# One transformer pair on one core: the first down projection by one level of Strassen's product, with weight sums made in DRAM

## The chip, the core and the metric

The kernel runs on one core of one Trainium2 chip. The metric is the device time of one execution in microseconds (us), the median of repeated executions. TensorE (PE) does the matrix products, VectorE (DVE) and ScalarE (ACT) the work on tiles, GpSimd (POOL) small side work, and the queue of SyncE (SP) issues every transfer of the kernel before. In the trace, PE is the matmul side of TensorE and PEld its loading of stationary operands.

## What is computed

Two blocks run one after the other on 512 tokens of width 1024 in float32. The first holds attention of 12 heads and a state-space mixer side by side; the part that matters here is its feed-forward at the end, and the attention at its start, because transfers of the change stand there.

```
f = rmsnorm(h, norm_ffn_pre_w[layer])
f = jnp.square(jax.nn.relu(f @ w_up[layer])) @ w_down[layer]      # 1024 -> 4096 -> 1024
h = h + rmsnorm(f, norm_ffn_post_w[layer])
```

The second block begins with a norm of h and its input projection, so the down projection `@ w_down` (4096 by 1024) stands between two stages that need all of its result.

## The kernel before

Every large product is done in three passes: each float32 operand is split into a high part (a cast on ACT, line 190) and the rest (a subtraction on DVE, line 191, or line 256 for activations), and PE multiplies high by high, high by rest and rest by high. One matmul has 128 rows of the contraction, 128 rows of the output and 512 columns. Line 151 is the one line from which all of them are issued.

The work is a list of units. A unit has a load (transfers on SP's queue into one of two raw buffers `wr`, then the split into slots `ws`) and a computation; `run_units` issues the loads two units ahead. Side work (softmax, norms, transposes) is cut into stages, which `poll` puts between matmuls. Last of all a scheduler sets the order of the instructions on each engine. It moves a transfer with no input to wait for far ahead: the two loads of norm weights `wpost` and `wpre`, which the program asks for after the state-space part, stand behind the loads of the first attention unit. Each engine, and SP's queue too, then runs its own list strictly in order: an instruction that waits holds all that stand behind it.

The feed-forward is cut into four slices of 1024 hidden channels. For each slice, units of `up_compute` make 256 hidden channels each, `relu_sq` (lines 1022 to 1028) applies the squared relu and splits the result, and then `tm_layer` (lines 966 to 1003) multiplies them by 1024 rows of `w_down`: two halves of the columns, four tiles of 128 tokens, eight blocks of contraction, three passes, which is 192 matmuls for a slice and 768 for the layer. Each of the 32 tiles of PSUM is added to `o` in SBUF (line 958; the first slice by a copy on ACT, line 956). In the last slice the tiles are in the order of `TILE_ORDER`, so that tokens 0 to 255 are complete when half of the unit is done. `finish` then does the norms for one tile of 128 tokens, and `to_fm` transposes it on PE (line 155) for the next stage, `u_first`. That one works in two halves, tokens 0 to 255 first (`split_run`).

In the attention, each of six units `qk_compute` loads 1 MB (`wqk0` to `wqk5`, two transfers each, q weights first), makes q and k for a pair of heads, and starts the softmax as side work. Four units with gate weights (`wga0` to `wga3`) and four with the attention's projection (`wap`) follow, then the state-space part. There POOL multiplies the tiles `Cp` (line 755).

Of the kernel before, what the change touches and what calls it, by code (L numbers as in the profile page):

```python
# [8 lines left out]
F32 = mybir.dt.float32  # L9
# [5 lines left out]
P = 128  # L15
S = 512
# [57 lines left out]
def kernel(  # L74
# [67 lines left out]
            n *= d  # L142
        return n

    def mm(o, lhsT, rhs, start, stop):
# [5 lines left out]
        pe.matmul(o, lhsT=lhsT, rhs=rhs, start=start, stop=stop)  # L151

    def tr(o, i, idn):
        cost(0.109)
# [89 lines left out]
    def tm_mm(ps, ws, xf, t, kx0=0, first=True, last=True):  # L244
        n = len(ws)
        for i, (hi, lo) in enumerate(ws):
            xh = xf(kx0 + i, 0)[:, t * P:(t + 1) * P]
            xl = xf(kx0 + i, 1)[:, t * P:(t + 1) * P]
            mm(ps, lhsT=xh, rhs=hi, start=first and i == 0, stop=False)
            mm(ps, lhsT=xh, rhs=lo, start=False, stop=False)  # L250
            mm(ps, lhsT=xl, rhs=hi, start=False, stop=last and i == n - 1)
            poll()

    def split_fm(dst, src):
# [399 lines left out]

    def gate_compute(kind, i):
        def f(ws):
            for m in range(2):
                ps = ps_tile(f"g{kind}{i}_{m}")
                fm_mm(ps, ws[m], XU, KK8)
# [11 lines left out]

    def att_proj(i):
        def f(ws):
            require(*[held["att", pr] for pr in range(6)])
            for m in range(2):
                ps = ps_tile(f"ap{i}_{m}")
# [138 lines left out]

    def x_compute(g):
        def f(ws):
            xF = N.gp.tile([P, 2, S], F32, tag="xF", name=f"xF{g}")
            for b in range(2):
                ps = ps_tile(f"px{g}_{b}")  # L820
# [4 lines left out]

    def bc_compute(g):
        def f(ws):
            for j, nm in enumerate("BC"):
                t = N.gp.tile([P, S], F32, tag=nm, name=f"{nm}{g}")
                ps = ps_tile(f"p{nm}{g}")  # L830
# [4 lines left out]

    def z_compute(g):
        def f(ws):
            zs = N.gp.tile([P, 2, S], F32, tag="zs", name=f"zs{g}")
            for b in range(2):
                ps = ps_tile(f"pz{g}_{b}")  # L840
# [4 lines left out]

    def half_proj(i):
        def f(ws):
            require(*[held["ssd", g] for g in range(4)])
            for m in range(2):
                ps = ps_tile(f"sp{i}_{m}")  # L850
# [32 lines left out]

    def ssm_proj(i):
        def f(ws):
            for m in range(2):
                b = 2 * i + m
                ga = N.gtp.tile([P, S], F32, tag="ga", name=f"ga{b}")
# [131 lines left out]
    R = {}  # L1020

    def relu_sq(ps, m):
        rt = N.rtp.tile([P, S], F32, tag="rt", name=f"rt{m}")
        act.activation(rt, ps, AF.Relu)  # L1024
        dve.tensor_mul(rt, rt, ps)  # L1025
        r = N.rp.tile([P, 2, S], F32R, tag="r", name=f"r{m}")
        split_fm(r, rt)
        R[m] = r

    def open_ffn():  # L1030
        mxs.close()
        pools(ffn, ("rp", 12), ("rtp", 2))

    def up_first(ws):
        open_ffn()
        for m, ps in enumerate(split_run(ws, "U2", "upf")):
            relu_sq(ps, m)

    def up_compute(i):
        def f(ws):  # L1040
            for m in range(2):
                ps = ps_tile(f"up{i}_{m}")
                fm_mm(ps, ws[m], u_acc(N.U), KK8)
                relu_sq(ps, 2 * i + m)
        return f

    def up_between(si):
# [20 lines left out]

    def open_b2():
        ffn.close()  # L1070
        N.extra = None
        nts.close()
        outs.close()
# [427 lines left out]
```

## Time and profile before

| | us |
|---|---|
| median of 3 runs | 1754.76 (1753.95 to 1755.08) |
| the profiled execution: its own time | 1755.96 |
| the profiled execution: span of the core, first to last instruction | 1754.2 |
| PE busy in it | 1733.7 (99%) |
| DVE / ACT / POOL busy in it | 938.0 / 815.5 / 133.3 |
| granted clock of TensorE, mean over the span | 0.997 of full speed |

The profiled execution took 1.76 us more than its span, and 1.2 us more than the median of the three runs. PE is busy nearly always, so a change pays by fewer matmuls and costs by each wait that it puts in front of one. The transfers use the 16 DMA engines for 31.8% of the span on the mean, but not evenly.

### The profile page before, as it was taken

To read this page: it belongs to the slowest core of one execution; us is meant where nothing else is said; L and a number is where in the kernel's file an instruction comes from. 1 tells how busy PE (TensorE), PEld (TensorE's weight loads), DVE (VectorE), ACT (ScalarE), POOL (GpSimd) and SP (SyncE) were. 2 spreads that over 40 slices of the span, in tenths; PEclk is the share of its full clock that TensorE was granted. 3 is DMA by queue.
4 is the path that set the end of the run, shared out by engine and by line. 5 is a ranking of instruction groups with operands and counts; after the bars stand their busy time and mean duration, and the time that the engine had idled before them with its cause. 6 is when DMAs were issued, how large, how long until landed. Compare 5 with 4: busy or idle time off the path is not lost.

```text
span 1754.2 us, 21065 instructions
## 1 busy us (share of the span) xinstructions
PE 1733.7 (99%) x8517; PEld 1434.3 (82%) x8517; DVE 938.0 (53%) x1328; ACT 815.5 (46%) x1302; POOL 133.3 (8%) x125
## 2 busy tenths in 40 slices
PE   8999999999999999999999999999999999999998
PEld 7877788888888888898888888887779888888887
DVE  5676445677346756563334344699846432333363
ACT  5656526777457774343323232445474323222242
POOL 1000000111001110000000000144301000000000
PEclk9999999999999999999999999999999999999999
DMA  7411153222332236342323231423233433333311
GB/s 233 112 51 61 39 166 97 72 73 73 108 97 72 73 102 210 112 165 72 121 72 120 72 118 50 141 76 97 84 121 97 144 96 97 96 96 96 134 59 49
DMA packets 179403, 176.44 MB, mean 101 GB/s; under 512 B 5665, under 2 KB 148073, under 8 KB 179178
## 3 DMA queue, kind: packets, MB, share of 16 engines
q1 hardware_dynamic: 179306, 175.10, 31.8%
q8 instruction: 67, 1.10, 0.3%
q14 instruction: 30, 0.25, 0.0%
HBM read 166.69 MB, written 8.39 MB: 100 GB/s over the span
## 4 chain that ended last, share of the span: by engine, by line
PE 93%; ACT 2%; DVE 2%; issue 1%; POOL 1%; DMA 1%; SPq 0%; POOLq 0%; DVEq 0%; ACTq 0%
PE dn L151 10%; PE up L151 9%; PE d L151 7%; PE gg L151 6%; PE gu L151 6%; PE g L151 5%; PE pz L151 5%; PE px L151 5%; PE wo L151 4%; PE v L151 3%; PE ple L151 3%; PE pB L151 2%; PE sq L151 2%; PE sp L151 2%; PE pC L151 2%; PE ap L151 2%
## 5 line engine op out<-in xcount | busy, mean ns | idle before, releaser
L151 PE MATMUL dn<-dnw_0s,r 128*128 128x512 f32 x384 | 94.0, 394 | 0.0
L151 PE MATMUL dn<-dnw_4s,r 128*128 128x512 f32 x384 | 93.3, 392 | 0.0
L151 PEld LDWEIGHTS dn<-dnw_0s,r 128*128 128x128 f32 x384 | 72.0, 188 | 16.4
L151 PEld LDWEIGHTS dn<-dnw_4s,r 128*128 128x128 f32 x384 | 72.1, 188 | 15.9
L1116 DVE SCALAR_TENSOR_TENSOR cv<-ucv,dwT,cv 128x512 f32<-128x512 f32 x100 | 74.9, 752 | 3.1 <-ACT cv L1111 0.9
L755 POOL TENSOR_TENSOR Cp<-Cp,C 128x384 f32<-128x384 f32 x32 | 32.5, 1015 | 518.4 <-ACT Cp L754 515.5
L151 PE MATMUL d<-d2w_0s,r 128*128 128x512 f32 x288 | 69.3, 389 | 0.0
L151 PEld LDWEIGHTS d<-d2w_0s,r 128*128 128x128 f32 x288 | 54.0, 188 | 11.2
L151 PE MATMUL d<-d2w_4s,r 128*128 128x512 f32 x240 | 58.5, 389 | 0.0
L151 PEld LDWEIGHTS d<-d2w_4s,r 128*128 128x128 f32 x240 | 45.0, 188 | 9.3
L752 DVE TENSOR_TENSOR M<-dec,cbm 128x512 f32<-128x512 f32 x32 | 27.7, 900 | 44.2 <-ACT dec L750 44.2
L958 DVE TENSOR_TENSOR dno<-dn,dno 128x512 f32<-128x512 f32 x24 | 16.5, 690 | 58.8 <-PE dn L151 58.8
L1024 ACT ACTIVATE rt<-up 128x512 f32<-128x512 f32 x28 | 16.7, 596 | 63.2 <-PE up L151 63.2
L1025 DVE TENSOR_TENSOR rt<-rt,up 128x512 f32<-128x512 f32 x28 | 19.2, 686 | 50.0 <-ACT rt L1024 50.0
L706 DVE SCALAR_TENSOR_TENSOR cvx<-px,convT,cvx 128x511 f32<-128x511 f32 (+2 forms) x48 | 35.7, 743 | 16.8 <-ACT cvx L704 16.4
L256 DVE TENSOR_TENSOR r<-rt,r 128x512 fp32r<-128x512 f32 x54 | 36.9, 686 | 6.9 <-ACT r L255 6.9
L1382 DVE TENSOR_TENSOR rt<-rt,gu 128x512 f32<-128x512 f32 x20 | 13.8, 688 | 49.9 <-PE gu L151 49.9
L749 ACT ACTIVATE dec<-R,acs 128x128 f32<-128x128 f32 x128 | 36.6, 378 | 8.0 <-PE R L151 8.0
L255 ACT CAST r<-rt 128x512 fp32r<-128x512 f32 x54 | 33.2, 617 | 14.3 <-DVE rt L1025 14.0
L1381 ACT ACTIVATE rt<-gg 128x512 f32<-128x512 f32 x20 | 11.9, 597 | 58.9 <-PE gg L151 58.9
L708 ACT ACT_TABLE_LOAD x15 | 19.2, 1283 | 28.3 <-DVE cvx L706 23.8
L191 DVE TENSOR_TENSOR dnw_4s<-dnw_4r,dnw_4s 128x1024 fp32r<-128x1024 f32 x16 | 19.6, 1225 | 22.9 <-ACT dnw_4s L190 22.9
(908 smaller groups left out, 4357.6 us busy)
## 6 DMA issues: line engine op xcount, KB each, us to landing
dnw_0r<-in_w_down_dram SPq DMA_DIRECT2D x8, 1024.0 KB
dnw_4r<-in_w_down_dram SPq DMA_DIRECT2D x8, 1024.0 KB, 4.9
d2w_0r<-in_w_ffn_down_dram SPq DMA_DIRECT2D x6, 1024.0 KB, 5.0
d2w_4r<-in_w_ffn_down_dram SPq DMA_DIRECT2D x4, 1024.0 KB, 5.1
x<-in_x_dram SPq DMA_DIRECT2D x4, 512.0 KB, 6.7
attd<-gt SPq DMA_DIRECT2D x8, 256.0 KB, 2.7
gsd<-gt SPq DMA_DIRECT2D x8, 256.0 KB, 2.0
wow_0r<-in_w_out_dram SPq DMA_DIRECT2D x2, 1024.0 KB, 6.2
```

What stands on the lines that cost most here:

```text
L151: pe.matmul(o, lhsT=lhsT, rhs=rhs, start=start, stop=stop)
L191: lo_eng["e"].tensor_sub(dst_lo, src, dst_hi)
L255: act.copy(dst[:, 0], src)
L256: dve.tensor_sub(dst[:, 1], src, dst[:, 0])
L706: dve.scalar_tensor_tensor(acc[:, j:], ps[:, :S - j], convT[:, (3 - j) * 32 + blk:(3 - j) * 32 + blk + 1], acc[:, j:], op0=ALU.mult, op1=A ...
L708: act.activation(dst, acc, AF.Silu)
L749: act.activation(dec[:, c, :], pr_[:, c * P:(c + 1) * P], AF.Relu, scale=-1.0, bias=acs[:, c, h:h + 1])
L752: dve.tensor_mul(M, dec, cbm)
L755: pool.tensor_mul(Cp, Cp, Cf[:, P:S])
L1024: act.activation(rt, ps, AF.Relu)
L1025: dve.tensor_mul(rt, rt, ps)
L1116: dve.scalar_tensor_tensor(ps, u_cv[b][:, k:k + S], wcol(k, b), ps, op0=ALU.mult, op1=ALU.add)
```

## The change

The product of a slice, 512 tokens by 1024 channels by 1024 columns, is cut into quarters: two halves of the tokens, two of the channels (even and odd blocks of 128), two of the columns. Eight products of quarters are replaced by seven (Strassen's method in Winograd's form), of which six have sums or differences of quarters as operands on one or both sides.

On the side of the activations, `pair_operands` makes four more combinations for every pair of blocks on DVE and splits seven operands of 256 tokens each. On the side of the weights, four sums t1 to t4 per slice are needed: t1 = B11 + B12, t3 = B22 + B12, t2 = t1 + B22, t4 = t2 + B21. They depend on the weights alone, and are built in DRAM long before: a copy from DRAM to DRAM issued on SP's queue (`copy`), and accumulating transfers issued by POOL (`add`), each in two halves of 512 KB. For the four slices this is 16 copies of 1 MB and 32 accumulating transfers of 512 KB. `behind()`, called at the start of 50 units from the attention to the state-space projection, hands out one of these 48 steps each time.

A product is 24 matmuls (two tiles of tokens, four blocks, three passes), its load one quarter of 1 MB, from `w_down` or from t1 to t4; seven products for each of four slices are 672 matmuls. Products n1, p6, p7 and p4 accumulate in one pair of PSUM banks, p5 and p3 in a second, p2 in a third, so that most products continue on what the one before left there, after it has been added to `o`.

The core of the diff (helpers that only pass an argument on are left out, and of the functions that now call `behind()` one is shown):

```diff
+    def split_negated(dst_hi, dst_lo, src):
+        act.activation(dst_hi, src, AF.Copy, scale=-1.0)
+        dve.scalar_tensor_tensor(dst_lo, src, -1.0, dst_hi, op0=ALU.mult, op1=ALU.subtract)
...
     def qk_compute(pr):
         def f(ws):
+            behind()
...
+    def quarters(w, k0, nk):
+        v = w[k0 * P:(k0 + nk) * P].rearrange("(j h p) c -> h p j c", h=2, p=P)
+        return {(i, j): v[i][:, :, 512 * j:512 * j + 512] for i in range(2) for j in range(2)}
+
+    def weight_sums(w, k0, nk, name):
+        B = quarters(w, k0, nk)
+        T = {}
+        for i in (1, 3, 2, 4):
+            t = spill.tile([nk // 2 * P, 512], F32, name=f"{name}t{i}")
+            T[i] = t.rearrange("(j p) c -> p j c", p=P)
+
+        def copy(i, src):
+            return [lambda: dma.dma_start(T[i], src)]
+
+        def add(i, src):
+            return [lambda j=j: pool.dma_start(T[i][:, j:j + 2], src[:, j:j + 2], accum_op=ALU.add)
+                    for j in range(0, nk // 2, 2)]
+
+        ops = (copy(1, B[0, 0]) + copy(3, B[1, 1]) + add(1, B[0, 1]) + add(3, B[0, 1]) + copy(2, T[1])
+               + add(2, B[1, 1]) + copy(4, T[2]) + add(4, B[1, 0]))
+        return B, T, ops
+
+    dn_sums = [weight_sums(w_down[0], 8 * s, 8, f"dn{s}") for s in range(4)]
+    background = []
+    for a, b in ((0, 1), (2, 3)):
+        for x, y in zip(dn_sums[a][2], dn_sums[b][2]):
+            background += [x, y]
+
+    def behind():
+        if background:
+            background.pop(0)()
...
-    tm_layer(w_out[0], [(0, 8)], lambda k, hl: MIX[k][:, hl, :], "U2", "wo")
+    tm_layer(w_out[0], [(0, 8)], lambda k, hl: MIX[k][:, hl, :], "U2", "wo", drop_extra=True)
...
+    def pair_operands(q, name):
+        dve.tensor_sub(q[:, 4:6], q[:, 1:2].to_broadcast([P, 2, 256]), q[:, 0:4:3])
+        dve.tensor_sub(q[:, 6], q[:, 0], q[:, 5])
+        dve.tensor_sub(q[:, 7], q[:, 2], q[:, 6])
+        X = N.xp.tile([P, 2, 7, 256], F32R, tag="X", name=name)
+        for a, b, n in ((0, 0, 1), (1, 2, 6)):
+            act.copy(X[:, 0, a:a + n], q[:, b:b + n])
+            dve.tensor_sub(X[:, 1, a:a + n], q[:, b:b + n], X[:, 0, a:a + n])
+        return X
...
+    PRODUCTS = (("n1", "A11", "B11", "x", ((0, 0, -1),)), ("p2", "A12", "B21", "v", ((0, 0, 1),)),
+                ("p5", "s1", "t1", "y", ((1, 1, 1),)), ("p3", "s4", "B22", "y", ((0, 1, 1),)),
+                ("p6", "s2", "t2", "x", ((0, 1, 1),)), ("p7", "s3", "t3", "x", ((1, 1, 1),)),
+                ("p4", "A22", "t4", "x", ((1, 0, -1),)))
+    LAST_OF = {(0, 0): "p2", (0, 1): "p6", (1, 0): "p4", (1, 1): "p7"}
...
+                for tt in range(2):
+                    ps = banks[si, bank][tt]
+                    tm_mm(ps, ws, lambda k, hl: pairs[k0 // 2 + k][:, hl, idx], tt, first=fresh, shared=True)
+                    for rh, ch, sign in uses:
...
+                        elif sign > 0:
+                            dve.tensor_add(sl, ps, sl)
+                        else:
+                            dve.tensor_sub(sl, sl, ps)
...
+    def relu_sq(pss, i):
+        q = N.qp.tile([P, 8, 256], F32, tag="q", name=f"q{i}")
+        for j, ps in enumerate(pss):
+            sl = q[:, 2 * j:2 * j + 2].rearrange("p a c -> p (a c)")
+            act.activation(sl, ps, AF.Relu)
+            act.activation(sl, sl, AF.Square)
+        XP[i] = pair_operands(q, f"x{i}")
...
-    tm_layer(w_down[0], [(8 * s, 8) for s in range(4)], lambda k, hl: R[k][:, hl, :], "U3", "dn", between=up_between,
-             drop_extra=True)
+    DN = [(8 * s, 8) for s in range(4)]
+    tm_strassen(w_down[0], dn_sums, DN, XP, "U3", "dn", up_between)
```

The scheduler does not keep the pace of `behind()`. All 16 copies and 32 accumulating transfers stand in the attention, ahead of its last units. Three places follow. In them `dn0t_417` is t1 of slice 0 in DRAM (418 is t3, 419 t2, 420 t4; slices 1, 2 and 3 have 421 to 424, 425 to 428 and 429 to 432), a name that ends in `r` is a raw buffer of weights, and what stands in brackets is what the row waits for: DMAHW is a transfer of SP's, DMASW one of POOL's.

The first place is SP's queue from the load of the first attention unit to that of the third, before:

```order
L207 DMA wqk0r<-in_w_in_dram 128x8x128 [waits DMAHW5_49,DVE_49]
L207 DMA wqk0r<-in_w_in_dram 128x8x128 [waits DMAHW6_49]
L177 DMA wpost_5834<-in_norm_mix_post_w_dram 128x1024 [waits DMAHW7_49]
L177 DMA wpre_5836<-in_norm_ffn_pre_w_dram 128x1024 [waits DMAHW0_49,PE_49]
L207 DMA wqk1r<-in_w_in_dram 128x8x128 [waits DMAHW1_49,DVE_49]
L207 DMA wqk1r<-in_w_in_dram 128x8x128 [waits DMAHW2_49]
L207 DMA wqk2r<-in_w_in_dram 128x8x128 [waits DMAHW5_49,DMAHW6_49,DMAHW3_49,DVE_49]
```

The same stretch of SP's queue in the changed kernel, from just behind the first copy:

```order
L709 DMA dn1t_421<-in_w_down_dram 128x4x512 [waits DMAHW0_49]
L211 DMA wqk1r<-in_w_in_dram 128x8x128 [waits DMAHW1_49,DVE_49]
L211 DMA wqk1r<-in_w_in_dram 128x8x128 [waits DMAHW2_49]
L709 DMA dn0t_418<-in_w_down_dram 128x4x512 [waits DMAHW3_49]
L709 DMA dn1t_422<-in_w_down_dram 128x4x512 [waits DMAHW4_49]
L709 DMA dn2t_425<-in_w_down_dram 128x4x512 [waits DMAHW5_49]
L709 DMA dn3t_429<-in_w_down_dram 128x4x512 [waits DMAHW6_49]
L709 DMA dn2t_426<-in_w_down_dram 128x4x512 [waits DMAHW7_49]
L709 DMA dn3t_430<-in_w_down_dram 128x4x512 [waits DMAHW0_49]
L177 DMA wpost_5898<-in_norm_mix_post_w_dram 128x1024 [waits DMAHW1_49]
L177 DMA wpre_5900<-in_norm_ffn_pre_w_dram 128x1024 [waits DMAHW2_49,PE_49]
L211 DMA wqk2r<-in_w_in_dram 128x8x128 [waits DMAHW3_49,DVE_49]
```

Eight copies of 1 MB have come in front of the load of `wqk2`, and POOL's first accumulating transfers run at the same time.

The second place is ACT's list around the cast of the q half of `wqk2`. Before, it stands among the copies of v, ahead of the first q of all:

```order
L557 COPY vT<-v_2_493 128x256 [waits PE_49]
L190 CAST wqk1s_436<-wqk1r 128x1024 [waits DMAHW2_49,DVE_49,PE_49]
L190 CAST wqk2s_571<-wqk2r 128x1024 [waits DMAHW3_49,DVE_49,PE_49]
L557 COPY vT<-v_3_520 128x256 [waits PE_49]
L190 CAST wqk2s_574<-wqk2r 128x1024 [waits DMAHW4_49,DVE_49]
```

In the changed kernel it stands behind the copies of the first k (`kk`) and ahead of those of the second q (`qs_0_700`) and of the first exponentials of the softmax (`sc`):

```order
L648 CAST kk_1_597<-k_642 64x512 [waits DVE_49]
L649 CAST kk_1_597<-k_642 64x512
L190 CAST wqk2s_587<-wqk2r 128x1024 [waits DMAHW3_49]
L643 CAST qs_0_700<-q_704 64x512 [waits PE_49]
L190 CAST wqk2s_590<-wqk2r 128x1024 [waits DMAHW4_49]
L643 CAST qs_1_701<-q_704 64x512 [waits DVE_49]
L599 ACTIVATE sc_722,ls_724<-sc_722,mx_723 128x128 [waits DVE_49]
```

It has moved from well ahead of its use to just before it, and the first softmax now stands behind it. On DVE the matching subtraction has moved likewise, ahead of the first row maxima.

The third place is SP's queue at the gate weights. Before, nothing stands between the loads:

```order
L207 DMA wqk5r<-in_w_in_dram 128x8x128 [waits DMAHW6_49,DMAHW5_49,DVE_49]
L207 DMA wqk5r<-in_w_in_dram 128x8x128
L207 DMA wga0r<-in_w_in_dram 128x8x256 [waits DMAHW7_49,DMAHW0_49,DVE_49]
L207 DMA wga1r<-in_w_in_dram 128x8x256 [waits DMAHW2_49,DMAHW1_49,DVE_49]
L207 DMA wga2r<-in_w_in_dram 128x8x256 [waits DMAHW3_49,DVE_49]
```

In the changed kernel:

```order
L709 DMA dn2t_427<-dn2t_425 128x4x512 [waits DMASW1_49,DMASW0_49]
L709 DMA dn3t_431<-dn3t_429 128x4x512 [waits DMASW3_49,DMASW2_49]
L211 DMA wqk5r<-in_w_in_dram 128x8x128 [waits DMAHW6_49,DMAHW5_49,DVE_49]
L211 DMA wqk5r<-in_w_in_dram 128x8x128
L211 DMA wga0r<-in_w_in_dram 128x8x256 [waits DMAHW2_49,DMAHW7_49,DMAHW1_49,DVE_49]
L211 DMA wga1r<-in_w_in_dram 128x8x256 [waits DMAHW5_49,DMAHW6_49,DMAHW0_49,DVE_49]
L709 DMA dn0t_420<-dn0t_419 128x4x512 [waits DMASW1_49,DMASW0_49]
L709 DMA dn1t_424<-dn1t_423 128x4x512 [waits DMASW3_49,DMASW2_49]
L709 DMA dn2t_428<-dn2t_427 128x4x512 [waits DMAHW3_49,DMASW5_49,DMASW4_49]
L709 DMA dn3t_432<-dn3t_431 128x4x512 [waits DMAHW4_49,DMASW7_49,DMASW6_49]
L211 DMA wga2r<-in_w_in_dram 128x8x256 [waits DMAHW7_49,DVE_49]
```

Copies that wait for accumulating transfers have come in front of loads; the last of them, t4 of slice 3, waits for the 24th of POOL's 32 transfers, and `wga2` and all later loads stand behind it. POOL's own list has all 32 in a row, ahead of its first multiplication of `Cp`.

## Rows read from the trace of the kernel before

**Rows 1.** Page, parts 1 and 4: busy time of PE; the chain by engine.

```profile
PE 1733.7 (99%) x8517; PEld 1434.3 (82%) x8517; DVE 938.0 (53%) x1328; ACT 815.5 (46%) x1302; POOL 133.3 (8%) x125
...
PE 93%; ACT 2%; DVE 2%; issue 1%; POOL 1%; DMA 1%; SPq 0%; POOLq 0%; DVEq 0%; ACTq 0%
```

**Rows 2.** Groups by line: matmuls of the down projection (count; busy us, mean ns).

```profile
L151 PE MATMUL dn<-dnw_0s,r 128*128 128x512 f32 x384 | 94.0, 394 | 0.0
L151 PE MATMUL dn<-dnw_4s,r 128*128 128x512 f32 x384 | 93.3, 392 | 0.0
```

**Rows 3.** The chain in order of time: slices of both down projections (start, us).

```profile
813.86 44.23 PE dn L151 x192
...
1568.66 43.52 PE d L151 x192
```

**Rows 4.** Groups by line, 814 to 1113 us: DVE and ACT (mean ns last).

```profile
L191 DVE TENSOR_TENSOR dnw_4s<-dnw_4r,dnw_4s 128x1024 fp32r<-128x1024 f32 x13 | 15.9, 1225 | 19.3 <-ACT dnw_4s L190 19.3
L958 DVE TENSOR_TENSOR dno<-dn,dno 128x512 f32<-128x512 f32 x23 | 15.9, 690 | 58.8 <-PE dn L151 58.8
...
L1024 ACT ACTIVATE rt<-up 128x512 f32<-128x512 f32 x23 | 13.7, 596 | 50.5 <-PE up L151 50.5
L190 ACT CAST dnw_4s<-dnw_4r 128x1024 fp32r<-128x1024 f32 x13 | 13.6, 1047 | 16.6 <-PE up L151 16.6
```

**Rows 5.** Windows: busy us of each engine, clock, DMA share, GB/s, an up stage.

```profile
858.00:902.00 44.00, 44.00 (x194) 36.17 (x193) 19.89 (x23) 16.02 (x23) 0.00 (x0) 1.00 0.36 120
```

**Rows 6.** Transfers by issue: KB each, median us from issue to landing.

```profile
dnw_4r<-in_w_down_dram SPq DMA_DIRECT2D x8, 1024.0 KB, 4.9
...
gsd<-gt SPq DMA_DIRECT2D x8, 256.0 KB, 2.0
...
gs<-gsd SPq DMA_DIRECT2D x8, 256.0 KB, 3.1
...
d2w_4r<-in_w_ffn_down_dram SPq DMA_DIRECT2D x2, 512.0 KB, 3.7
```

**Rows 7.** Timeline of PE and DVE behind the last tile of the layer (start, us).

```profile
1110.10 2.88 PE L151 MATMUL dn<-dnw_4s,r 128*128 128x512 f32 x12
...
1125.93 1.04 PE L155 MATMUL dnf<-c_sb,dno 128*128 128x128 f32 x8
1127.21 0.39 PE L151 MATMUL u2f<-U,w2a0s 128*128 128x256 f32 x1 [0.24 <-ACT U L309]
```

**Rows 8.** Windows of 5 us in the attention's start: DMA share, GB/s last.

```profile
27.00:32.00 5.00, 5.00 (x28) 4.23 (x27) 2.01 (x3) 1.66 (x3) 0.00 (x0) 1.00 1.10 334
32.00:37.00 5.00, 5.00 (x28) 4.37 (x27) 0.37 (x1) 1.26 (x2) 0.00 (x0) 1.00 1.06 316
37.00:42.00 5.00, 5.00 (x29) 4.42 (x29) 3.22 (x4) 3.66 (x5) 0.00 (x0) 1.00 0.17 43
42.00:47.00 5.00, 5.00 (x40) 5.00 (x39) 1.50 (x3) 0.75 (x2) 0.00 (x0) 1.00 0.79 210
```

**Rows 9.** Timeline of SP's queue: when two loads were issued.

```profile
41.40 0.99 SPq L207 DMA_DIRECT2D wqk2r<-in_w_in_dram  x2
...
113.97 0.37 SPq L207 DMA_DIRECT2D wga2r<-in_w_in_dram  x1
```

**Rows 10.** Timeline of PE, DVE and ACT at the places where the change waits.

```profile
78.44 4.70 PE L151 MATMUL q<-U,wqk2s 128*128 128x512 f32 x20
82.98 0.27 PE L155 MATMUL pt<-c_sb,sc 128*128 128x128 f32 x1
...
129.00 1.40 PE L151 MATMUL q<-U,wqk5s 128*128 128x512 f32 x5
...
70.14 0.42 DVE L588 CUSTOM_DVE_ANT_0 sc<-S,G 128x256 f32<-128x256 f32 x1 [1.17 <-PE S L151]
...
146.40 0.58 ACT L638 CAST qs<-q 64x512 fp32r<-64x512 f32 x1 [3.38 <-PE S L151]
148.44 0.58 ACT L643 CAST kk<-k 64x512 fp32r<-64x512 f32 x1 [1.46 <-PE k L151]
```

**Rows 11.** Timeline of POOL: its first multiplication in the state-space part.

```profile
287.32 1.01 POOL L755 TENSOR_TENSOR Cp<-Cp,C 128x384 f32<-128x384 f32 x1 [267.06 <-ACT Cp L754]
```

More of the change, by code (lines that the diff above doesn't have):

```diff
@@ L242, in fm_mm, with tm_mm @@
             poll()
-    def tm_mm(ps, ws, xf, t, kx0=0, first=True, last=True):
+    def tm_mm(ps, ws, xf, t, kx0=0, first=True, last=True, shared=False):
         n = len(ws)
@@ L248, in tm_mm @@
             xl = xf(kx0 + i, 1)[:, t * P:(t + 1) * P]
-            mm(ps, lhsT=xh, rhs=hi, start=first and i == 0, stop=False)
-            mm(ps, lhsT=xh, rhs=lo, start=False, stop=False)
-            mm(ps, lhsT=xl, rhs=hi, start=False, stop=last and i == n - 1)
+            mm(ps, lhsT=xh, rhs=hi, start=first and i == 0, stop=False, shared=shared)
+            mm(ps, lhsT=xh, rhs=lo, start=False, stop=False, shared=shared)
+            mm(ps, lhsT=xl, rhs=hi, start=False, stop=last and i == n - 1, shared=shared)
             poll()
@@ L656, in f @@
         def f(ws):
+            behind()
             for m in range(2):
@@ L827, in f @@
         def f(ws):
+            behind()
             for j, nm in enumerate("BC"):
@@ L885, in f @@
         def f(ws):
+            behind()
             for m in range(2):
@@ L1014, in split_run, with load_q, f @@
         return pss
-    tm_layer(w_out[0], [(0, 8)], lambda k, hl: MIX[k][:, hl, :], "U2", "wo")
-    ffn = ExitStack()
[L1020 to L1028, printed above, removed]
+    tm_layer(w_out[0], [(0, 8)], lambda k, hl: MIX[k][:, hl, :], "U2", "wo", drop_extra=True)
+    def load_q(src, nk, name, negated=False):
+        def f():
+            raw = wrp.tile([P, 2048], F32, tag="wr", name=f"{name}r")
+            rv = raw[:, :nk * 512].rearrange("p (k c) -> p k c", k=nk)
+            dma.dma_start(rv, src)
+            res = []
+            for k in range(0, nk, 2):
+                m = min(2, nk - k)
+                sl = slot(f"{name}s{k}")
+                v = sl[:, :, :m * 512].rearrange("p h (k c) -> p h k c", k=m)
+                (split_negated if negated else split_weights)(v[:, 0], v[:, 1], rv[:, k:k + m, :])
+                res += [(v[:, 0, j, :], v[:, 1, j, :]) for j in range(m)]
+            return res
+        return f
@@ new lines, with tm_strassen, product, f @@
+    PRODUCTS = (("n1", "A11", "B11", "x", ((0, 0, -1),)), ("p2", "A12", "B21", "v", ((0, 0, 1),)),
[3 more added lines that the diff above has]
+    LAST_OF = {(0, 0): "p2", (0, 1): "p6", (1, 0): "p4", (1, 1): "p7"}
+    def tm_strassen(w, sums, slices, pairs, key, name, between):
+        o, ss = {}, {}
+        last = len(slices) - 1
+        seen = set()
+        def product(si, prod, banks):
+            pname, a, _, bank, uses = prod
+            idx = XI[a]
+            k0, nk = slices[si]
+            def f(ws):
+                fresh = (si, bank) not in banks
+                if fresh:
+                    banks[si, bank] = [ps_tile(f"{name}{si}{bank}{tt}") for tt in range(2)]
+                for tt in range(2):
+                    ps = banks[si, bank][tt]
+                    tm_mm(ps, ws, lambda k, hl: pairs[k0 // 2 + k][:, hl, idx], tt, first=fresh, shared=True)
+                    for rh, ch, sign in uses:
+                        t = 2 * rh + tt
+                        if t not in o:
+                            o[t] = N.op.tile([P, D], F32, tag=f"o{t}", name=f"{name}o{t}")
+                        hs = slice(512 * ch, 512 * ch + 512)
+                        sl = o[t][:, hs]
+                        if (t, ch) not in seen:
+                            seen.add((t, ch))
+                            if sign > 0:
+                                act.copy(sl, ps)
+                            else:
+                                act.activation(sl, ps, AF.Copy, scale=-1.0)
+                        elif sign > 0:
+                            dve.tensor_add(sl, ps, sl)
+                        else:
+                            dve.tensor_sub(sl, sl, ps)
+                        if si == last and LAST_OF[rh, ch] == pname:
+                            junk = N.ntp.tile([P, 512], F32, tag="junk", name=f"{name}j{ch}{t}")
+                            ss[t, ch] = square_sum(sl, junk, f"{name}{ch}{t}")
+                            dve.tensor_mul(sl, sl, N.wpost[:, hs])
+                            if (t, 1 - ch) in ss:
+                                u_ready[key, t] = side(finish(t, o[t], [ss[t, 0], ss[t, 1]], N.wpre, N.U, name))
+            return f
+        for si, (k0, nk) in enumerate(slices):
+            between(si)
+            B, T, _ = sums[si]
+            banks = {}
+            for prod in PRODUCTS:
+                wn = prod[2]
+                src = B[int(wn[1]) - 1, int(wn[2]) - 1] if wn[0] == "B" else T[int(wn[1])]
+                unit(load_q(src, nk // 2, f"{name}w{si}{prod[0]}", prod[0] in ("n1", "p4")), product(si, prod, banks))
@@ L1034, in up_first @@
     def up_first(ws):
         open_ffn()
-        for m, ps in enumerate(split_run(ws, "U2", "upf")):
-            relu_sq(ps, m)
+        pss = split_run(ws, "U2", "upf")
+        for i in range(2):
+            relu_sq(pss[2 * i:2 * i + 2], i)
     def up_compute(i):
         def f(ws):
+            pss = []
             for m in range(2):
```

18 lines of the change are left out of this document (12 added, 6 removed).

## The prediction, made before the changed kernel ran

> **What bounds the kernel now.** I read the page first: PE is busy for 1733.7 us, 99% of the span, and the chain of work that ended last is 93% PE [rows 1]. So the time falls by the matmuls that go, and rises by every wait put in front of one. Then the groups by line, for what the change removes: the down projection is 768 matmuls, in two groups of 384 [rows 2]. Their mean of 392 to 394 ns is the length of one in the pipeline; what one costs is its pitch, and that the chain shows: the last slice of this layer takes 44.23 us for 192 matmuls, the like slice of the second layer 43.52 [rows 3], 230.4 and 226.7 ns. I take the smaller, since the other holds waits. Third, the costs of what DVE and ACT do for a product [rows 4], and the stretch of an up stage for how full they are: DVE busy 19.9 of 44 us, ACT 16.0, the transfers at a share of .36 [rows 5]. Last, since the new transfers stand in the attention, the windows of its start [rows 8], the issues of the loads behind them [rows 9], and when their data is used [rows 10].
>
> **The matmuls.** 28 products of 24 are 672 in place of 768: 96 × 226.7 ns = **−21.8 us**. The clock is at full speed in every window shown, so the pitch stays.
>
> **The products' pace.** A product is 24 × 226.7 ns = 5.44 us of PE. For each, a quarter of 1 MB is loaded: 193 GB/s, against 334 where the transfers are saturated [rows 8]. It is split in two parts, ACT 2 × 1.05 = 2.1 us, DVE 2 × 1.23; two evacuations of 0.69 are added on DVE, which makes 3.8 of 5.44 us [rows 4]. So each keeps pace, DVE with little left. A raw buffer is used by every second product: landing 4.9 [rows 6], 1.05, 2 × 1.23 are 8.4 of 10.9 us; it binds when a transfer takes some 2.5 us longer. Within a slice, three times a product starts on a bank that the one before must first have emptied (p3 on p5's, p7 on p6's, p4 on p7's). Two tiles alternate, so the wait is what one evacuation and its queue on DVE exceed 12 matmuls, 2.7 us: mostly nothing, up to some 2 us when a split of 1.23 and the pair sums stand ahead. The pair sums and splits of activations come in the up stages, where DVE has half its time free [rows 5]; it is this half that hides them. Only for the last pair of the last slice is there no stage behind it. Bounds: 0 where all is covered, 1 us for each of the 12 reuses above. I take a third, **+4** (0 to 12).
>
> **The end of the layer.** Before, the next stage's first matmul is at 1127.21, 14.2 us behind the last tile's end at 1112.98 (the norm of a tile, its transposes `dnf`, a copy) [rows 7]; in that time PE has other tiles to run only if the order has them. In the changed order tokens 0 to 255 are complete with p6, and behind it run p7 and p4, 48 matmuls or 10.9 us, on which the finish of the first two tiles is hidden. 14.2 − 10.9 leaves 3.3 us; the finish also queues behind the evacuations of p7 and p4 on DVE. Without a queue and with a shorter chain it is 0; with the whole finish of a second tile behind, 10. I take **+5**.
>
> **The transfers in the attention.** This is the term that decides. Nothing in the trace copies from DRAM to DRAM or accumulates, so I bound both.
>
> A copy of 1 MB: 3.1 us if it is one pass at 334 GB/s, 6.3 if it is a read and then a write. A store of 256 KB lands in 2.0 us, no later than a load of 256 KB in 3.1 [rows 6]; writing is not the slower side, and reads and writes of different packets can overlap. So nearer the lower: 4.0. By the Trainium skill, "DMA: Bandwidth & Descriptors", section "Latency and other measured facts", copies between HBM tensors ran at 207 to 214 GB/s at their full rate; 1 MB would be an estimated 4.9 us, and the total by that price 1783. No run here shows it yet.
>
> An accumulating 512 KB: engine time 1.6 us as one pass, 4.7 as three (two reads, one write, one after another). I take 2.4, one and a half passes. Landing alone 3.7 as the 512 KB load [rows 6] to 6.8 with three passes; I take 4.5, and 6 while copies run. That is 40% of the engines.
>
> First place: the load of `wqk2`. Before, it was issued at 41.40 [rows 9], when the queue had run empty at about 38 (share 1.06, then .17), and moved at 210 GB/s [rows 8]. Now eight copies stand ahead. Its q half of 512 KB needs 2.5 us at that rate and 1.8 of latency (4.9 − 3.1), so it lands L = 38 + (8 × 4.0 + 4.3) / 0.6 = 98. Before, it was first used at 78.44, by `q` on PE. Its cast and its subtraction now stand on ACT and DVE ahead of the copies of the second q and of the first row maxima, which began at 70.14 and release the transposes `pt` at 82.98 [rows 10]. So all behind 70 is held on both engines, and PE soon after it, since the PSUM tiles of the scores are not read. The stall is L − 70 = 28 us; cast and subtraction, 2.3 us, are inside the uncertainty. Bounds: with copies of 3.1 us and accumulations that use only time left free, L = 67 and the stall is 0. With copies of 6.3 and accumulations of 4.7 out of 8.3 us, L = 38 + 54.7 / 0.43 = 165, the stall 95.
>
> The copies of t2 ahead of `wqk4` and `wqk5` wait for the 4th and the 12th accumulating transfer, about 62 and 107 by these prices, so that `wqk5` lands by 120; its first use was at 129 before any shift [rows 10], so they hold nothing more.
>
> Second place: `wga2`. On SP's queue it stands behind a copy that waits for the 24th accumulating transfer. By 98, ten are done (60 / 6); fourteen more at 4.5 end at 161, two copies of 4.0 and a landing of 4.9 make 174. The cast of `wga2` now stands on ACT between the copies of the sixth q and k, 146.40 and 148.44 before [rows 10]; before, the load was issued at 113.97 [rows 9]. 174 − 147 = 27, nearly the 28 by which all has already been shifted, so the two are one term: the larger. **+28** (0 to 95).
>
> Behind the 24th are eight more transfers on POOL, until about 200. POOL's first multiplication `Cp` comes at 287.32 after 267 us of idling [rows 11], so that list has cover of over 80 us and costs nothing; were it used up, each us late there would hold the state-space part. Reading t1 to t4 comes hundreds of us later.
>
> **Sum**, against the profiled execution's own 1755.96 us: −21.8 + 4 + 5 + 28 = +15.2, so 1771.2; that execution was 1.2 us above the median of the runs, which makes **1770**, slower by 0.9%. About 3.5 us, 0.2%, is what a measurement of this kernel can tell from no change.
>
> **The rivals.**
>
> *The transfers are hidden (faster).* Without the third term: 1755.96 − 21.8 + 9 − 1.2 = 1742. For it: the kernel's own mean use of the transfers is low, a window at a share of .17 stands just there [rows 8], and `wqk2` landed long before its use. Against it: eight copies need 25 us at the lowest price, five such windows. It decides at a stall of 13 us, that is `wqk2` landed by 83 and `wga2` by 160. The first holds with copies of 4.0 if accumulations take under a fifth of the engines: 38 + 36.3 / 0.8 = 83. With copies of 3.1 they may take 35%. Chance .34.
>
> *Accumulation is read twice, one after the other.* Each 512 KB then holds the engines for 3.1 us and takes 4.5 + 0.8 = 5.3, and 7 beside copies. L = 38 + 36.3 / 0.56 = 103, nine are done, and fifteen of 5.3 end at 183; with 12.9 for copies and landing, `wga2` is there at 196, 49 us behind its place. The time is 1791. It is SP's queue at the copies of t4 that decides. For it: an add needs the old value too; against it: nothing shows that the reads cannot run beside writes. Chance .17. The Trainium skill says so of another transfer, in "Collectives: The Full Stack", section "The bandwidth ceiling: the fold count and why AG ≠ RS ≠ AR": an add needs two source reads from one ring, so that a reduce ran at about half the rate of a copy. No run here shows it yet.
>
> *The products don't keep pace (no gain).* If DVE is late in each product by 1 us, 28 us are lost in place of 4, and with hidden transfers the time is 1766. What speaks for it is 3.8 of 5.44 us on DVE, with sums for `o` and splits in one list; against it, that a second slot of weights is ready ahead. It decides at 0.6 us a product. Chance .05.
>
> *About even*, a stall of 9 to 16 us, 1751 to 1758: .08.
>
> **How the numbers follow.** The forecast has .36: it needs a stall of 17 to 45 us, its own range is 1759 to 1787, and middle values of both prices give it, as would copies of 6 us with nothing else beside them (L = 90). Slower is .36 + .17 + .05 = .58, the same .08, faster .34. Faster runs spread from 1736 (waits near their lower ends) to 1751; the second rival to 1820. The range 1738 to 1815 leaves about 2 in 10 out, on both sides together: the upper bounds of both prices lie above it.
>
> **What the profile will show.** Right, if line 151 has 672 of these matmuls at the same pitch; PE idles between 70 and 110 us, its releasers being ACT's cast of `wqk2` and behind it a transfer of SP's queue; `wqk2` lands near 98, the t1 and t3 copies near 4 us each when spread over their number; `wga2` is issued behind a wait on POOL's transfers at about 170; the clock stays at full speed outside the idle time; `Cp` isn't late against its own stage. In the products single waits of 1 to 2 us stand on the DVE evacuation, and one of some 5 us ahead of `u2f`.
>
> Wrong, if the attention's start shows no idle time on PE (then transfers are cheaper than the middle, and the first rival is right), if `wga2` alone is late (accumulation was mis-sized, not the copy), if PE's idle time in the products is over 12 us, or if a load is late at another place, since accumulations slow all loads from 40 to 200 us, those of `wqk3` to `wga1` too.

## The result, and the profile of the changed kernel

The changed kernel takes **1825.26 us** (median of 4 runs, 1824.13 to 1827.06) against 1754.51 beside it: ratio 1.0404, 95% interval 1.0386 to 1.0422. It is slower, as forecast, but by 71 us where the forecast had 15, and the time lies above the range.

The table has the start of the first matmul of some stages, in us, from the timelines of PE.

| first matmul of | before | changed | difference |
|---|---|---|---|
| transposes `pt` of the first softmax | 82.98 | 90.15 | +7.2 |
| gate weights, `g` | 148.24 | 183.63 | +35.4 |
| attention's projection, `ap` | 214.79 | 303.42 | +88.6 |
| up stage, `up` | 769.95 | 858.67 | +88.7 |
| down projection | 813.70 | 902.37 | +88.7 |
| next stage, `u2f` | 1112.82 | 1185.99 | +73.2 |

The whole loss comes between 83 and 303 us, in three pieces of 7, 28 and 53 us. The feed-forward then gives 15.5 us back. From there to the end the difference shrinks by only 2 us more, to the 71 of the medians.

The page of the changed kernel: busy times, the queue of POOL's transfers (packets, MB, share of the time of 16 engines), the chain of work by engine.

```profile
PE 1715.7 (94%) x8421; PEld 1419.3 (78%) x8421; DVE 993.3 (54%) x1392; ACT 866.3 (47%) x1358; POOL 169.5 (9%) x157
...
q0 software_dynamic: 8704, 16.78, 5.5%
...
PE 83%; issue 7%; ACT 3%; DMA 3%; DVE 3%; POOL 2%; SPq 0%; POOLq 0%; DVEq 0%; ACTq 0%
```

Against [rows 1], PE has 96 matmuls less and 18 us less work, and its share has gone from 99% to 94%. In the chain, 7% is "issue": an engine that waits for nothing the profile shows. Whose it is, the chain in order of time says (start, us, what):

```profile
57.46 21.50 DMA wqk2r<-in_w_in_dram
...
79.39 1.14 POOL dn0t L712
80.52 8.79 issue
89.32 1.16 POOL dn0t L712
...
98.87 1.15 POOL dn1t L712
...
104.83 1.15 POOL dn1t L712
105.98 4.82 issue
110.80 1.15 POOL dn2t L712
...
209.16 7.12 issue
...
216.29 5.66 DMA dn3t<-in_w_down_dram
...
222.65 11.29 DMA wga2r<-in_w_in_dram
```

From 79 to 222 us the chain is POOL and its transfers alone: it issues an accumulating transfer in some 1.15 us and then stands for 4.6 to 8.8 us before the next. The first four issues lie ahead of this chain, 9 to 12 us apart, beside the copies on SP's queue (POOL's timeline):

```profile
36.68 1.33 POOL L712 DMA_DIRECT2D dn0t<-in_w_down_dram  x1 [16.91 <-DMA dn0t<-in_w_down_dram]
45.90 1.17 POOL L712 DMA_DIRECT2D dn0t<-in_w_down_dram  x1 [7.89 <-issue]
57.14 1.14 POOL L712 DMA_DIRECT2D dn1t<-in_w_down_dram  x1 [10.08 <-issue]
69.35 1.15 POOL L712 DMA_DIRECT2D dn1t<-in_w_down_dram  x1 [11.06 <-issue]
```

Later POOL stands even where the engines have room. Two windows show it, the first without a copy (the length; PE, PEld, DVE, ACT and POOL with busy us and instructions; then clock, transfers' share, GB/s):

```profile
100.00:120.00 20.00, 20.00 (x106) 16.29 (x105) 14.78 (x38) 11.33 (x27) 3.47 (x4) 1.00 0.56 88
200.00:220.00 20.00, 0.00 (x0) 0.00 (x0) 0.00 (x0) 0.00 (x0) 3.45 (x3) 0.50 0.62 125
```

The transfers' share is .56 and .62, far from the 1.06 to 1.10 of [rows 8]. In the second window PE, DVE and ACT do nothing at all. SP's queue shows what is held meanwhile:

```profile
57.46 11.92 SPq L211 DMA_DIRECT2D wqk2r<-in_w_in_dram  x2
...
78.95 1.35 SPq L709 DMA_DIRECT2D dn0t<-dn0t  x1
...
122.49 0.54 SPq L709 DMA_DIRECT2D dn2t<-dn2t  x1
137.23 0.54 SPq L709 DMA_DIRECT2D dn3t<-dn3t  x1
137.87 1.19 SPq L211 DMA_DIRECT2D wqk5r<-in_w_in_dram  x2
...
178.84 0.54 SPq L709 DMA_DIRECT2D dn0t<-dn0t  x1
...
222.01 0.53 SPq L709 DMA_DIRECT2D dn3t<-dn3t  x1
222.65 0.57 SPq L211 DMA_DIRECT2D wga2r<-in_w_in_dram  x1
```

The copy of t2 of slice 3 goes out at 137.23 and the load of `wqk5` behind it; the copy of t4 of slice 3 goes out at 222.01, and `wga2`, issued at 113.97 before [rows 9], at 222.65. ACT's casts of these weights show the three holds (duration; idle before, and what ended it):

```profile
78.99 1.04 ACT L190 CAST wqk2s<-wqk2r 128x1024 fp32r<-128x1024 f32 x1 [12.45 <-DMA wqk2r<-in_w_in_dram]
...
147.25 1.04 ACT L190 CAST wqk5s<-wqk5r 128x1024 fp32r<-128x1024 f32 x1 [30.72 <-DMA wqk5r<-in_w_in_dram]
...
233.96 1.04 ACT L190 CAST wga2s<-wga2r 128x1024 fp32r<-128x1024 f32 x1 [51.63 <-DMA wga2r<-in_w_in_dram]
```

PE waits behind all three (waits of PE from 60 to 300 us: total, times, longest):

```profile
PE pt L155 <- DVE sc L604: 50.8, 3, 50.1
PE o L151 <- ACT PT L618: 25.7, 1, 25.7
PE q L151 <- ACT qs L643: 5.8, 1, 5.8
```

That is 82.3 of the 88.6 us. Around such a wait the granted clock is lower too: .50 in the second window above, in which PE stood still, which is the lower of its two levels, 1.2 GHz; .84 from 240 to 260, where the matmuls begin again; 1.00 from 260 on.

At the end of the layer (PE, start and us) the first finished tile's transposes are there at once, and for the second's PE waits 8 us:

```profile
1169.52 5.60 PE L151 MATMUL dn3x<-dnw3p4s,x 128*128 128x512 f32 x24
1175.10 1.10 PE L155 MATMUL dnf<-c_sb,dno 128*128 128x128 f32 x8
1184.20 1.97 PE L155 MATMUL dnf<-c_sb,dno 128*128 128x128 f32 x8 [8.00 <-DVE dno L986]
```

### The profile page after: what moved, and what is told of

Same layout as the page of the kernel before. It is cut to its first block, busy times and chain, and to the rows that moved or that the text cites. A ratio compares the mean times of both kernels' runs of the same rounds, so it can differ in the third digit from the quotient of the medians.

```text
span 1825.3 us, 21137 instructions
## 1 busy us (share of the span) xinstructions
PE 1715.7 (94%) x8421; PEld 1419.3 (78%) x8421; DVE 993.3 (54%) x1392; ACT 866.3 (47%) x1358; POOL 169.5 (9%) x157
## 3 DMA queue, kind: packets, MB, share of 16 engines
q1 hardware_dynamic: 194090, 204.46, 35.4%
q0 software_dynamic: 8704, 16.78, 5.5%
## 4 chain that ended last, share of the span: by engine, by line
PE 83%; issue 7%; ACT 3%; DMA 3%; DVE 3%; POOL 2%; SPq 0%; POOLq 0%; DVEq 0%; ACTq 0%
PE up L151 8%; PE d L151 7%; PE gg L151 6%; PE gu L151 6%; PE pz L151 5%; PE px L151 5%; PE g L151 5%; PE wo L151 4%; PE v L151 3%; PE ple L151 2%; PE pB L151 2%; PE sq L151 2%; PE sp L151 2%; PE pC L151 2%; PE ap L151 2%
## 5 line engine op out<-in xcount | busy, mean ns | idle before, releaser
L155 PE MATMUL pt<-c_sb,sc 128*128 128x128 f32 x120 | 17.9, 284 | 50.8 <-DVE sc L604 50.8
L155 PEld LDWEIGHTS pt<-c_sb,sc 128*128 128x128 f32 x120 | 14.4, 143 | 54.4 <-DVE sc L604 51.9
L1090 DVE TENSOR_TENSOR x<-q,x 128x256 fp32r<-128x256 f32 (+1 forms) x32 | 34.7, 1088 | 23.1 <-ACT x L1089 23.1
L151 PE MATMUL o<-PT,vT 128*64 128x256 f32 (+3 forms) x96 | 22.0, 461 | 25.7 <-ACT PT L618 25.7
L1089 ACT CAST x<-q 128x256 fp32r<-128x256 f32 (+1 forms) x32 | 29.7, 942 | 34.0 <-DVE q L1086 23.4
L151 PEld LDWEIGHTS o<-PT,vT 128*64 128x64 f32 x96 | 9.0, 139 | 33.4 <-ACT PT L618 26.1
L1158 ACT ACTIVATE q<-up 128x512 f32<-128x512 f32 x28 | 16.6, 592 | 37.0 <-PE up L151 37.0
L599 ACT ACTIVATE sc<-sc,mx 128x128 f32<-128x128 f32 (+3 forms) x48 | 26.4, 552 | 11.3 <-DVE mx L595 11.1
```

Source lines behind the costliest of these rows:

```text
L151: pe.matmul(o, lhsT=lhsT, rhs=rhs, start=start, stop=stop, skip_group_check=shared)
L155: pe.transpose(o, i, idn)
L599: act.activation(sl, sl, AF.Exp, bias=mx[:, i:i + 1], accum_out=ls[:, i:i + 1])
L1089: act.copy(X[:, 0, a:a + n], q[:, b:b + n])
L1090: dve.tensor_sub(X[:, 1, a:a + n], q[:, b:b + n], X[:, 0, a:a + n])
L1158: act.activation(sl, ps, AF.Relu)
```

## The experiments

The first four were to tell apart: the products, the transfers as such, SP's waits for POOL, and POOL's pace.

**Products without sums** (`e1_products_only`). T stands for the sums in DRAM; each is replaced by a quarter of the weights.

```diff
-                src = B[int(wn[1]) - 1, int(wn[2]) - 1] if wn[0] == "B" else T[int(wn[1])]
+                src = B[int(wn[1]) - 1, int(wn[2]) - 1] if wn[0] == "B" else B[{1: (0, 0), 2: (1, 1), 3: (1, 1), 4: (1, 0)}[int(wn[1])]]
...
-            background += [x, y]
```

> This run leaves out the building of the sums: in place of t1 to t4 the products read one quarter of the weights each (so the output is not the layer's), with the same bytes, splits, matmuls and evacuations, and no transfer is added to the attention. Theory (the products give their gain, and the whole loss stands in the attention): behind the attention the changed kernel gained 73.2 of the 88.7 us back that it had lost by the start of the up stage, 15.5 us net, so about 1739 us (1736 to 1743). Rival (the products are slowed by waits of their own, or the gain was only work catching up behind the stall): 1748 us or more.

1739.49 us, ratio 0.9911 (0.9896 to 0.9926). `u2f` begins at 1097.52, 15.3 us earlier than before. The products give about what their matmuls promise, less the 8 us of waiting at the layer's end, which this run has too: −21.8 + 8.0 is −13.8, measured −15.

**Transfers without products** (`e2_transfers_only`). The kernel before, with the functions of the change that build the sums and one call of `behind()` in each of the same units.

```diff
     def qk_compute(pr):
         def f(ws):
+            behind()
```

> The kernel before with the 16 copies and 32 accumulating transfers added and their sums read by nobody; SP's and POOL's queues in the attention are those of the changed kernel. Theory (the attention's transfers are the whole loss, and what they cost does not depend on the products): 1754.5 + 88.6 = 1843 us (1838 to 1848). Rival (part of the 88.6 us is other: the moved casts, or the products' raw buffers): below 1835.

1839.44 us, ratio 1.0483 (1.0465 to 1.05); `up` begins at 853.35, 83.4 us late. So the transfers cost 83 to 85 us with no product to read them, a little less than the 88.6 beside the products. Of the two expectations the theory's holds. The two runs on both sides of the change, −15 and +85, add up to 70 of the 71 measured.

**Addends swapped** (`e3_swapped`).

```diff
-        ops = (copy(1, B[0, 0]) + copy(3, B[1, 1]) + add(1, B[0, 1]) + add(3, B[0, 1]) + copy(2, T[1])
-               + add(2, B[1, 1]) + copy(4, T[2]) + add(4, B[1, 0]))
+        ops = (copy(1, B[0, 0]) + copy(3, B[1, 1]) + add(1, B[0, 1]) + add(3, B[0, 1]) + copy(2, B[1, 1])
+               + add(2, T[1]) + copy(4, B[1, 0]) + add(4, T[2]))
```

> The two addends of t2 and t4 change places: the copy takes the plain quarter, the accumulating transfer adds t1 or t2. Same sums, same number and size of transfers, but no copy on SP's queue waits for POOL any more; all 16 copies then stand ahead of wqk2. Theory (the loss is SP's queue held behind accumulating transfers that run one at a time, 6 us each): the holds before wqk5 (about 25 us) and wga2 (about 55) go, and wqk2, which landed at 79 behind eight copies, lands behind sixteen, 40 to 50 us later: about 1785 us (1770 to 1800). Rival (the DMA engines are simply full, whoever waits for whom): the same work has to pass before the last load, and the time stays within 10 us of 1825.

1773.86 us, ratio 1.0106 (1.0091 to 1.0121): 51 us come back with the same bytes moved. One wait is left, at the first place, where `wqk2` now stands behind sixteen copies in place of eight (waits of PE, 60 to 260 us):

```profile
PE q L151 <- ACT wqk2s L190: 31.3, 1, 31.3
```

That the DMA engines are simply full is refuted. POOL's transfers still went one at a time here, the last issued at 270.59; with no copy on SP's queue waiting for them, that pace held no load.

**Twice the descriptor space** (`e4_scratch`).

```diff
-dynamic_dma_scratch_size=1024
+dynamic_dma_scratch_size=2048
```

> The changed kernel with twice the scratch space for the descriptors of POOL's transfers (2048 in place of 1024 bytes), every engine's order as in the changed kernel. Theory (POOL issues one accumulating transfer only when the one before has landed, because its descriptors fill the space, and that is what sets 6 us): two are in flight, one passes every 3.5 to 4.5 us, the 24th is done by about 150 in place of 222, and the time falls to 1750 to 1775 us. Rival (one accumulating transfer takes that long in the engines, or POOL waits for something else): within 5 us of 1825.

1781.89 us, ratio 1.0153 (1.0137 to 1.0168), a little above the expected span; 43 us come back. POOL now issues two in one go and then waits for landings (POOL's timeline; x2 are two issues):

```profile
35.63 2.51 POOL L712 DMA_DIRECT2D dn0t<-in_w_down_dram  x2 [15.42 <-DMA dn0t<-in_w_down_dram]
...
163.08 2.31 POOL L712 DMA_DIRECT2D dn0t<-in_w_down_dram  x2 [21.56 <-DMA dn0t<-dn0t]
...
188.43 1.14 POOL L712 DMA_DIRECT2D dn3t<-in_w_down_dram  x1 [2.55 <-issue]
```

The last of the 32 is issued at 188.43, in the changed kernel at 272.81. The copy that waits for the 24th goes out at 156.32 in place of 222.01. So the space for descriptors, which held one transfer, set the pace. What is lost now is lost at the first place: with accumulations two at a time beside them, the eight copies are slower to leave SP's queue, the load of `wqk2` goes out at 73.48 in place of 57.46, and PE waits 31.8 us behind its cast, where it had waited 5.8 (SP's timeline; waits of PE).

```profile
156.32 2.01 SPq L709 DMA_DIRECT2D dn3t<-dn3t  x1
...
PE q L151 <- ACT qs L643: 31.8, 1, 31.8
```

The Trainium skill, "DMA: Bandwidth & Descriptors", section "SWDGE vs HWDGE vs iDMA", says that for transfers issued from GpSimd the descriptors are written into rings in a part of SBUF set aside for them. This run agrees in that the size of such a space decides how many are in flight; where the space lies, no run here shows.

Two more runs priced the parts.

**Copies alone** (`e6_copies_only`).

```diff
-        ops = (copy(1, B[0, 0]) + copy(3, B[1, 1]) + add(1, B[0, 1]) + add(3, B[0, 1]) + copy(2, T[1])
-               + add(2, B[1, 1]) + copy(4, T[2]) + add(4, B[1, 0]))
+        ops = (copy(1, B[0, 0]) + copy(3, B[1, 1]) + copy(2, T[1]) + copy(4, T[2]))
```

> All accumulating transfers are left out, the 16 copies stay (the sums are then wrong: t1 is B11 and so on); ten copies stand ahead of wqk2, none waits for POOL. Theory (a copy of 1 MB takes the engines 3 to 4 us, and it is the accumulations that cost): wqk2 lands at 67 to 75, no stall or one of 2 us, 1739 to 1744 us. Rival (the copies are the main load): wqk2 at 85 or later, 1755 us or more.

1744.7 us, ratio 0.9949 (0.9934 to 0.9964), 0.7 us above the expected span: `wqk2` is cast at 73.0, `g` begins 5.4 us late. Of SP's queue the page of this run shows

```profile
q1 hardware_dynamic: 194090, 204.46, 37.2%
```

and that of the products without sums, which has the same loads and no copy,

```profile
q1 hardware_dynamic: 185642, 187.68, 34.3%
```

37.2% of 1742.6 us less 34.3% of 1738.3 are 52 us for 16 copies: **3.3 us** of all engines for 1 MB, if the loads took the same in both. Two windows in which little but copies is on the queue fit this (share and GB/s last):

```profile
40.00:45.00 5.00, 5.00 (x38) 4.92 (x37) 2.79 (x4) 2.25 (x4) 0.00 (x0) 1.00 1.06 354
45.00:50.00 5.00, 5.00 (x40) 5.00 (x39) 0.39 (x2) 0.75 (x2) 0.00 (x0) 1.00 1.07 335
```

**Half the bytes added** (`e7_half_adds`).

```diff
-            return [lambda j=j: pool.dma_start(T[i][:, j:j + 2], src[:, j:j + 2], accum_op=ALU.add)
+            return [lambda j=j: pool.dma_start(T[i][:, j:j + 1], src[:, j:j + 1], accum_op=ALU.add)
```

> Each of the 32 accumulating transfers adds one block of 256 KB in place of two (half of each sum is left out); the number of transfers, the copies and the waits of SP's queue stay. Theory (one at a time; of the 6 us between two, some 3.2 are the engines' work on 512 KB, and the rest is latency and issue): 4.2 to 4.7 us between two, the 24th done near 160 in place of 222, 1762 to 1785 us. Rival 1 (the pace is a fixed cost for each transfer): 6 us stay, above 1810 us. Rival 2 (it is all by the byte): 3 us, the 24th before 130, 1740 to 1755 us.

1763.3 us, ratio 1.006 (1.0043 to 1.0077). The time is in the span of the theory, but by another path, so that the hit is luck. The 24th transfer was issued at 120.18 and had landed by 129.97, when the copy that waits for it went out. The theory had it near 160; before 130 was the sign of rival 2. The one wait of PE, 21.6 us, stands at the first place, where `wqk2` is cast at 89.44. Nor does the run show the split into engine work and latency: two of the smaller transfers are in flight at once, as POOL's timeline shows, so that with their size the number that the space holds was changed too.

```profile
35.94 1.86 POOL L712 DMA_DIRECT2D dn0t<-in_w_down_dram  x2 [16.14 <-DMA dn0t<-in_w_down_dram]
38.29 0.81 POOL L712 DMA_DIRECT2D dn1t<-in_w_down_dram  x1 [0.49 <-DMA dn1t<-in_w_down_dram]
...
120.18 0.82 POOL L712 DMA_DIRECT2D dn3t<-in_w_down_dram  x1 [3.46 <-issue]
```

What it gives is the work by the byte: the queue's share is halved.

```profile
q0 software_dynamic: 4608, 8.39, 2.8%
```

2.8% of 1761.2 us over 32 are 1.5 us for 256 KB; 5.5% of 1825.3 over 32 are **3.1 us** for 512 KB.

Then I tried to keep the gain. **Copies held back by data** (`e5_gated`): a transfer of one value out of a unit's result into a corner of the copy's target orders the copy behind that unit.

```diff
+    def behind(src):
+        c, steps = background.pop(0)
+        dma.dma_start(c, src[0:1, 0:1])
+        for f in steps:
+            f()
...
+            if pr >= 2:
+                behind(kk[0].bitcast(F32))
...
+            behind(acc)
...
+            if i in (2, 4, 6, 8):
+                behind(XP[i][:, 0, 0].bitcast(F32))
```

> The addends swapped as in the run before, and each copy held back by data: a transfer of 4 bytes writes a value of the unit just computed into a corner of the copy's target, so that the copy cannot start before that unit. Slices 1 and 0 are built unit by unit behind the last q and k units and the gate units of the attention, slices 2 and 3 behind the units of the state-space projection and the up stages. Same sums, same number and size of copies and accumulations. Theory (the loss came from where the transfers stood on the queues, not from their bytes): the attention's start is as before, and the time is that of the products alone, 1739.5, plus at most a few us for the small transfers: 1739 to 1747 us. Rival (33 MB more traffic costs wherever it stands, or POOL's transfers hold Cp): 1755 us or more.

1751.36 us (10 runs, 1747.86 to 1755.31), ratio 0.9986 (0.9976 to 0.9996): faster than before by 0.1%, between theory and rival. The attention is whole (`ap` at 214.74, `wo` at 709.33), but `up` begins at 781.05, 11.1 us late. The norms of the stage ahead need a small multiplication on POOL, line 298, and four accumulating transfers now stand among these (POOL's timeline, and the row of DVE that waits):

```profile
737.18 1.14 POOL L716 DMA_DIRECT2D dn2t<-dn2t  x1 [4.95 <-issue]
...
742.86 1.19 POOL L716 DMA_DIRECT2D dn2t<-dn2t  x1 [1.25 <-issue]
749.08 1.14 POOL L716 DMA_DIRECT2D dn2t<-dn2t  x1 [5.02 <-issue]
749.79 1.03 POOL L298 TENSOR_TENSOR woq1r<-woq1v,neghalf 128x1 f32<-128x1 f32 x1
...
750.85 1.28 DVE L984 SCALAR_TENSOR_TENSOR woo<-h,woq1r,wpre 128x1024 f32<-128x1024 f32 x1 [5.45 <-POOL woq1r L298]
```

So a transfer that waits for descriptor space holds POOL's own work too.

**Away from the norms** (`e8_moved`): slices 2 and 3 wholly in the up stages. The edit is shown against the held-back version.

```diff
-            behind(acc)
...
-            if i in (2, 4, 6, 8):
+            if 2 <= i <= 9:
```

> The held-back version again, with the eight steps of slices 2 and 3 behind eight units of the up stages (the third to the tenth), none behind the state-space projection. Theory (the 11 us that the held-back version lost stood at the norms ahead of the up stage, where POOL's small multiplications for the norm wait behind its accumulating transfers, and nowhere else): the products' gain stays whole, 1739.5 us, 1738 to 1744. Rival (the added traffic costs wherever it stands): the loss moves into the up stages and the products, and the time stays at 1748 us or more.

**1739.45 us**, ratio 0.9910 (0.9893 to 0.9926), the time of the products without any transfer. Of PE's waits none is left in the attention or at the norms ahead of the up stage; the largest of the run is the one at the layer's end:

```profile
PE dnf L155 <- DVE dno L983: 8.0, 1, 8.0
```

**The same with the first addends** (`e9_not_swapped`). The edit is shown against the version just before.

```diff
-               ((1, B[0, 0], B[0, 1]), (3, B[1, 1], B[0, 1]), (2, B[1, 1], T[1]), (4, B[1, 0], T[2]))]
+               ((1, B[0, 0], B[0, 1]), (3, B[1, 1], B[0, 1]), (2, T[1], B[1, 1]), (4, T[2], B[1, 0]))]
```

> The same, with the addends as in the changed kernel: the copies of t2 and t4 read t1 and t2 and wait on SP's queue for POOL again, 15 us or more behind POOL's issue. Theory (the wait costs only where POOL has a backlog of transfers that run one at a time; when one unit's transfers are done before the next unit's, nothing is held): the same time within 3 us. Rival (a wait of SP for POOL holds loads in any case): slower by 8 us or more.

1739.31 us, ratio 0.9907 (0.9892 to 0.9922). In the attention SP now hardly waits for POOL, 1.4 us in all between 120 and 215 us, because each unit's transfers are done before the next copy is asked for. One long wait is left in the feed-forward, in front of loads of the products (waits of SP's queue, 770 to 1000 us):

```profile
SPq L713 <- DMA dn2t<-in_w_down_dram: 10.9, 1, 10.9
```

The load of `dnw1p5` behind it goes out at 882.32, in the version before at 876.72, and PE does not wait for it. So a wait of SP for POOL cost nothing where it was short or where the loads behind it were early enough; it cost where POOL had a backlog.

## Why the prediction was wrong

The sign was right, and so was the mechanism in its form: the matmuls give their 21.8 us, and transfers hoisted into the attention take it back at the loads behind them. What failed is one term, +28, which was 88.6, and in it the pace of the accumulating transfers.

- **The step that failed** is the second place: "By 98, ten are done (60 / 6); fourteen more at 4.5 end at 161". Beside copies one accumulating transfer took not 6 but 8.3 to 12.2 us from issue to issue, and alone not 4.5 but 5.8 to 6.3. By 98 six were done, not ten: the seventh was issued at 98.87. The 24th, issued at 216.29, was done at 222 in place of 161. With 222 the prediction's own sum, 12.9 us for copies and landing less the place at 147, gives 88, so the rest of the term was sound. I had taken one transfer at a time without asking what makes it so; the doubled space shows that it is the room for descriptors. Landing is then the pace, and all of what slows a landing is multiplied by 24. Of the prediction's signs of being wrong the nearest was a `wga2` that is late because accumulation was mis-sized.
- **The engine time** I took as 2.4 us was 3.1, the value of the rival in which the old value is read in addition. That rival's price was right, and its sum, 1791, was too low for the same reason as mine. That the old value's read is what the time goes to is not shown: against the copies alone, the page of the changed kernel counts 16.78 MB more read and 16.78 MB more written, one read for each byte added. Nor does any run say what the rest of the 5.8 us from issue to issue is. The Trainium skill, "Collectives: The Full Stack", section "The bandwidth ceiling: the fold count and why AG ≠ RS ≠ AR", has a reduce at about half the rate of a copy; here 512 KB in 3.1 us are 167 GB/s, half of the 334 of [rows 8], and a copy's 1 MB in 3.3 us is 318. The ratio agrees; its reason, one ring for both reads, no run here shows.
- **"So they hold nothing more"**, of `wqk4` and `wqk5`, was wrong: the 12th transfer was done at 137, when the copy that waits for it went out, and not at 107, and `wqk5` was cast at 147.25. This middle hold made 28 of the 88.6 us.
- **The first place** was oversized: copies took the engines 3.3 us, not 4.0, and fewer accumulations ran beside them. `wqk2` landed at 79, not 98, and cost 7 us, not 28. The Trainium skill, "DMA: Bandwidth & Descriptors", section "Latency and other measured facts", has 207 to 214 GB/s for copies between HBM tensors, of tiles with rows of 16 KiB. That is not what these copies show, with 318 by the engines' time and 335 to 354 in the two windows of the copies alone; the measurement decides.
- **"So the two are one term"** holds in its form: what the first holds shifted counts again at the last. `wga2`'s cast came at 233.96, 87 us behind its place, and that is the loss.
- **The products' pace**, +4, measured 0.3 us of waits in the feed-forward. **The end of the layer**, +5, measured 8.0. There I had misread [rows 7]: the matmul of `u2f` at 1127.21 is not its first, which began at 1112.82, so the 14.2 us lie beside other matmuls, and PE waited for only 0.5 us there before. The 3.3 us taken from them came near by luck; the queue on DVE, which the prediction names as well, is what the trace shows. The second of the two first tiles, not the first, is late on DVE, behind p7's and p4's evacuations and the splits of the next stage.
- **`Cp`** was free as said: it begins at 375.96, 88.6 us later like all else, and 102 us behind the last accumulating transfer.
- The faster rival had .34, and its case is a real one: 1742 was forecast for hidden transfers, and 1739.4 is what two versions with the same transfers in other places take.

## What to carry to other kernels

Before a transfer that others wait for goes on a queue, ask how many of its kind can be in flight. If it is one, as here, its price is its landing time multiplied by the number that stand ahead, not its bytes. A chain of such transfers must be kept off an in-order queue that also issues the loads, or be spread so that each link is done before the next is asked for. A background transfer needs something that holds it back as well as something that waits for it: the scheduler here, which saw no input, moved such transfers to the front, where they competed with the loads that are needed first.

## What the runs showed of the hardware that I had not expected

POOL stands still while an accumulating transfer waits for descriptor space, 4.6 to 5.1 us for each where little else moved and up to 11 beside copies; small multiplications for a norm, queued behind such transfers, made the next stage 11 us late. Accumulating 512 KB from DRAM into DRAM took the engines 3.1 us, a plain copy of 1 MB 3.3.
